# Loading the pooling weights sooner and closing a gate's sums later in a hybrid transformer block

## The chip, the cores and the metric

The kernel runs on one core of a Trainium2 chip. The metric is the time of one execution on the device in microseconds (us); the median of several runs is used. All times inside an execution are counted from the start of its span, the stretch from its first to its last recorded instruction.

## The reference

One layer of a backbone works on 1024 latent tokens and 256 context tokens with 1024 features each, in 32-bit floats. What matters here:

```python
mod_x = silu(c) @ w_mod + b_mod                  # shifts, scales and gates: sh1 sc1 gt1 sh2 sc2 gt2
h_x, h_c = modulate(x, ...), modulate(ctx, ...)  # normalised, scaled, shifted
u, q, k, v = split(h @ w_in)                     # 512 columns each; k and v for the context as well
d = [window_mean(u_g, w) - u_g for w in (2, 4, 8, 16)]       # four groups of 128 channels
y = (d_g @ pool_w_g) * pool_scale                # a 128 x 128 weight per group
attn = neighbourhood_attention(q, k, v, k_ctx, v_ctx, rpb)   # 8 heads, softmax over a window and the context
mix = concat([y, attn]) @ w_out
x = x + gt1 * rmsnorm(mix, g_post_mix)           # the first gate
x = x + gt2 * rmsnorm(sq_relu_mlp(...), g_post_mlp)          # the second gate
```

The window means near both ends of the sequence have smaller counts; their reciprocals are the "table of ends".

## The kernel before

Every large product is made of three matmuls: each factor is split into a high part (a rounded copy, made by ScalarE, L146 or L148) and a low part (the rest, made by VectorE, L152 or L154), and L198, L199 and L200 multiply high by high, high by low and low by high. A weight's way is therefore: a DMA into one of four buffers ("raw"), a high part on ScalarE, a low part on VectorE, then its matmuls. Pages of 128 x 1024 floats come from a common pool of 33.

The stages that matter are these.

- Startup (up to L693): tokens are normalised and transposed, the pooling input u is projected, and the keys of the context are made (tiles `pkc`, copied by L690 to `kcT`). The last statement splits the values' weights `wv0` to `wv3`, whose DMAs were issued one by one as raw buffers came free. Inside this stage the order on TensorE, ScalarE, VectorE, SyncE's queue and GpSimd is the written order (`in_order`). Just ahead of the keys stand the loads of the pooling weights `pwt` (256 KB) and of the table of ends `edg` (32 KB), L636 to L640.
- The context's values (L731 to L743, tiles `pvc`), and then the latent tokens' values (`pv`). Between them VectorE makes the pooling differences (`pooled`, L643) and sums rows of the modulation (`accsh`, `accsc`), ScalarE splits the pooling weights into `pwh` and `pwl` (L739), and the pooling products follow (`py`). What stands in the block at L731 is only bound to come behind the last VectorE instruction of the startup.
- The query and key products (L916 to L946), in written order again. A part of this is the first gate: rows of `w_mod` are summed into `acca` on VectorE, then at step 17 `mod_gate` loads the gain `gpa` by four DMAs on SyncE's queue, sums over partitions with eight small matmuls (L236, tile `pga`) and multiplies (L244); `mod_out` sends the row out by four DMAs on GpSimd's queue (L250). Step 20 then calls `tables(0)`: its source is loaded as `U0w`, and GpSimd builds the bias tables for the first pair of heads out of it (L872).
- The attention, 32 units in rounds `i` (L1150 on), in written order on all engines. A round makes scores on TensorE (L978), adds bias and takes the minimum on VectorE (L992), the exponentials on ScalarE (L1001), transposes, and sums of values (L1054) for earlier units. `tables(1)` is called in round 2. The gate is read back as a page at round 30 (`gate_page`).
- The output projection, the MLP and the second gate, at whose start `mod_gate("b", ...)` loads a gain and closes the sums as well (L1869).

Of the kernel before, what the change touches and what calls it, by code (L numbers as in the profile page):

```python
# [18 lines left out]
P = 128  # L19
# [61 lines left out]
def hybrid_block(ctx, tc, x, ctx_in, w_mod, b_mod, gp1, gp2, w_in, pool_w, rpb, w_out, w1, w2, vectors,  # L81
# [94 lines left out]
    def load(name, src):  # L176
        raw = wraw.tile([P, 1024], F32, tag="raw", name=f"{name}w")
        nc.sync.dma_start(raw.rearrange("p (a b) -> p a b", b=src.shape[-1]), src)
        return raw
# [7 lines left out]
    def add_to(to, more):  # L187
        nc.gpsimd.dma_start(to, more, accum_op=add)

    def pair(w, kk, c0, n):  # L190
        return w[2 * kk * P : (2 * kk + 2) * P, c0 : c0 + n].rearrange("(a p) f -> p a f", p=P)
# [41 lines left out]
    def mod_sums_of(name, acc, bank):  # L233
        ps = bank(f"pg{name}")
        for c in range(4):
            nc.tensor.matmul(ps[32 * c : 32 * c + 32, :256], ones[:, :32], acc[:, c * 256 : (c + 1) * 256],  # L236
                             start=True, stop=True)
        return ps[:, :256]

    def mod_gate(name, acc, gp, bank, g):  # L240
        quarters = gp.rearrange("(c o f) -> c o f", c=4, o=1)
        for c in range(4):
            nc.sync.dma_start(g[32 * c : 32 * c + 32, :], quarters[c].to_broadcast([32, 256]))
        nc.vector.tensor_tensor(acc[:, :256], mod_sums_of(name, acc, bank), g, mul)  # L244


    def mod_out(name, acc):
        gates[name] = dram.tile([1, D], F32, tag=f"g{name}", name=f"g{name}")
        for c in range(4):
            nc.gpsimd.dma_start(gates[name][:, c * 256 : (c + 1) * 256], acc[32 * c : 32 * c + 1, :256])  # L250
# [17 lines left out]
    with tc.tile_pool(name="ps1", bufs=6, space=PSUM) as ps1, tc.tile_pool(name="tmp1", bufs=3) as tmp:  # L268

        def bank(name):  # L270
            if name[:2] == "pm" or name in ("pxt1_0", "pxt0_2", "pxt1_7", "pct2", "pct3"):
                return lasting(name)
            return ps1.tile([P, 512], F32, tag="mm", name=name)

        def once(name, shape):
            return tmp.tile(shape, F32, tag=name, name=name, bufs=1)
# [224 lines left out]
            return high_low(f"{name}{kk}", raw[kk], 1.0 if kk < 2 else -1.0)  # L501

        raw_k = [load(f"wk{kk}", pair(w_in, kk, 1024, 512)) for kk in range(KT // 2)]

# [126 lines left out]
        ctx_tok = lambda i: lambda k: (hc[k][0][:, i * P : (i + 1) * P], hc[k][1][:, i * P : (i + 1) * P])  # L633
        lat_tok = lambda b, i: lambda k: (hx[b][k][:, i * P : (i + 1) * P], hx[b][k][:, 512 + i * P : 512 + (i + 1) * P])

        pwt = once("pwt", [P, 4, P])  # L636
        nc.sync.dma_start(pwt, pool_w.rearrange("g c d -> c g d"))
        pwh, pwl = (tmp.tile([P, 512], F32R, tag=f"pw{n}", name=f"pw{n}", bufs=1) for n in "hl")
        edg = once("edg", [P, 4, 16])
        nc.sync.dma_start(edg, edge.rearrange("o (g e) -> o g e", g=4).to_broadcast([P, 4, 16]))  # L640
        dT = []

        def pooled(g, up):  # L643
# [84 lines left out]
        vcp = page("vc")  # L728
        pool_order = in_order(ET.Pool)
        pool_order.__enter__()  # L730
        with tc.issue_after(last[ET.DVE]):  # L731
            for i in range(2):
                ps = bank(f"pvc{i}")
                token_group(ps, wgt, ctx_tok(i))
                nc.scalar.copy(vcp[:, i * 512 : (i + 1) * 512], ps)
                if i == 0:
                    difference(1)
                    split(pwt.rearrange("p g d -> p (g d)"), pwh, pwl)
                    difference(2)  # L739
                else:  # L740
                    difference(3)
                background(2)
# [177 lines left out]
        with in_order(ET.PE, ET.Pool, ET.Activation, ET.DVE, ET.SP) as pooling:  # L920
            banks = {of: [bank(f"p{of}{j}") for j in range(2)] for of in "KQ"}
            use(-1)
            for step, (n, of, j) in enumerate([(n, of, j) for n, of in products for j in range(2)]):
                half_product(n, of, j, banks[of])
                use(step)
                if step in (5, 9, 17):
                    name = {5: "S1", 9: "S4", 17: "S3"}[step]
                    parts = token_operand(name, sraw[name])
                if step in (5, 7, 9, 11, 17, 19):
                    next(parts)  # L930
                    next(parts)
                if step in (7, 11):
                    name = {7: "S4", 11: "S3"}[step]
                    sraw[name] = token_raw(name)
                if step == 5:
                    column_sums("sc", accs["sc"], scale2)
                if step == 17:
                    mod_gate("a", accs["a"], gp1, bank, tmp.tile([P, 256], F32, tag="mrow", name="gpa", bufs=2))
                    mod_out("a", accs["a"])
                if step == 14:  # L940
                    mask_page()
                if step == 20:
                    tables(0)
                if step in (21, 22):
                    for g in range(2):
                        pool_mixed(2 * (step - 21) + g)  # L946
                kept_product(n, of, j, banks[of][j])


    with (  # L950
# [195 lines left out]
        with in_order(ET.PE, ET.Activation, ET.DVE, ET.SP) as projected:  # L1146
# [7 lines left out]
            for i in range(N + 4):  # L1154
                if i < N and units[i][1] == 2 and units[i][0] < 3:
                    tables(units[i][0] + 1)
                if i in LOADS:
                    weight_load(0, kks[LOADS.index(i)])
                if i == N:
                    t1 = [out_load(f"to1_{kk}w", kk, 1) for kk in (0, 1)]  # L1160
                    b22 = [out_load(f"bo22_{kk}w", kk, 1) for kk in (2, 3)]
                    t3 = [out_load(f"to3_{kk}w", kk, 1) for kk in (2, 3)]
                    for to, kk in zip(t1, (0, 1)):
                        add_to(halved(to), out_block(kk, 0))
                if i == N - 2:
                    G1 = gate_page("a")
                if i > 3:
                    weighed(i - 4)
                    if i % 8 == 3:
                        j = i // 8 - 1  # L1170
                        add_to(s1a[j], heads[j][:, 512:])
                        add_to(sa2[j], heads[j][:, 512:])
                if i in (1, 2):
                    with tc.issue_after(pooling[ET.Pool]):
                        for k in (2 * i - 2, 2 * i - 1):
                            add_to(s3[k], s1a[k])
                if i in (5, 6):
                    for k in (2 * i - 10, 2 * i - 9):
                        nc.sync.dma_start(sa2[k], s3[k])
                if 8 < i < N and i % 8 == 7:  # L1180
                    j = i // 8 - 1
                    add_to(heads[j][:, :512], sa2[j])
                low()
                if i > 0 and i % 8 == 0:
                    mixed_split(i // 8 - 1)
                for n, at in enumerate(HALVES):
                    if at == i:
                        weight_split(n)
                if i < N:
                    scores(i)  # L1190
                else:

                    t = i - N
                    if t == 0:
                        x, s1 = [], halves_of("so1_")
                    if t % 2 == 0:
                        xs = ps_s.tile([P, 1024], F32, tag="S", name=f"pox{t}")
                        x += [xs[:, :512], xs[:, 512:]]
                    out_sums(x[t], "A11", wo, t, True)
                    nc.scalar.copy(s1[t], x[t])  # L1200
                if 1 < i <= N + 1:
                    turn(i - 2)
                    fifth_kept(i - 2)
                if i < N:
                    exps(i, 0)
                if 1 < i <= N + 1:
                    turn_kept(i - 2, 0, nc.scalar.copy)
                if i < N:
                    exps(i, 1)
                if 1 < i <= N + 1:  # L1210
                    turn_kept(i - 2, 1, nc.vector.tensor_copy)
                if i < 2:
                    last_query("P4", i)
                if 0 < i <= N:
                    share(i - 1)
                if 2 < i <= N + 2:
                    values(i - 3)
                if i > N:
                    out_operand("S1", i - N - 1, s1a[i - N - 1])
# [25 lines left out]
    with tc.tile_pool(name="ps2", bufs=6, space=PSUM) as ps2:  # L1245
# [6 lines left out]
      with ExitStack() as tmp2:  # L1252
# [550 lines left out]
        with tc.issue_after(first[ET.PE]), in_order(ET.PE, ET.Activation, ET.DVE, ET.SP):  # L1803
# [59 lines left out]


            pg = bank("pgb")
            x = four("pyx")
            for g in range(NG):
                if g == 2:
                    acc = acc_b[-1]  # L1869
                    mod_gate("b", acc, gp2, lambda name: pg, tmp.tile([P, 256], F32, tag="gp", name="gpb", bufs=1))  # L1870
                    mod_out("b", acc)
                group(x, "P1", g)
            s1 = halves("s1")
            for t in range(4):
# [82 lines left out]
```

## Time and profile before

| | us |
|---|---|
| median of 3 runs | 1038.9 |
| lowest and highest | 1038.55, 1040.34 |
| the profiled execution | 1039.78 |
| its span | 1038.0 |
| TensorE busy | 1020.5 |
| VectorE busy | 755.6 |
| ScalarE busy | 543.5 |
| GpSimd busy | 107.8 |

In a profile PE is TensorE, PEld its loading of weights, ACT ScalarE, DVE VectorE, POOL GpSimd, SPq SyncE's queue. A row of the timeline gives start, duration, engine, line, operation, tile written and tiles read, shapes and count; in square brackets stands how long the engine was idle before it and who ended that. A row of the waits gives who waited for whom, the time in total, how often, and the longest. A row of the windows gives the stretch, its length, the busy time of each engine with the number of instructions, the granted clock of TensorE (1.00 is full speed), the busy share of the DMA engines and GB/s.

### The profile page before, as it was taken

To read this page: it belongs to the slowest core of one execution; us is meant where nothing else is said; L and a number is where in the kernel's file an instruction comes from. 1 tells how busy PE (TensorE), PEld (TensorE's weight loads), DVE (VectorE), ACT (ScalarE), POOL (GpSimd) and SP (SyncE) were. 2 spreads that over 40 slices of the span, in tenths; PEclk is the share of its full clock that TensorE was granted. 3 is DMA by queue.
4 is the path that set the end of the run, shared out by engine and by line. 5 is a ranking of instruction groups with operands and counts; after the bars stand their busy time and mean duration, and the time that the engine had idled before them with its cause. 6 is when DMAs were issued, how large, how long until landed. Compare 5 with 4: busy or idle time off the path is not lost.

```text
span 1038.0 us, 15636 instructions
## 1 busy us (share of the span) xinstructions
PE 1020.5 (98%) x5814; PEld 837.2 (81%) x5814; DVE 755.6 (73%) x1183; ACT 543.5 (52%) x941; POOL 107.8 (10%) x163
## 2 busy tenths in 40 slices
PE   8998999999999999999999999999999999999997
PEld 6787888877878888887888888888888888888885
DVE  5586937688997598868998888754586666547586
ACT  7572254318887556876555544544453334334431
POOL 3011121071211302310000000000000000000001
PEclk9998999999999999999999999999999999999999
DMA  9999598831337786794776657635698766545556
GB/s 341 329 246 339 191 228 291 277 81 62 72 93 193 167 189 203 225 254 164 258 267 222 213 203 226 210 112 206 239 335 277 235 233 221 203 175 193 174 185 206
DMA packets 122908, 221.63 MB, mean 214 GB/s; under 512 B 9424, under 2 KB 55248, under 8 KB 122832
## 3 DMA queue, kind: packets, MB, share of 16 engines
q1 hardware_dynamic: 96608, 170.75, 50.0%
q0 software_dynamic: 9088, 18.92, 9.4%
q10 hardware_dynamic: 17136, 30.97, 8.0%
q8 instruction: 45, 0.74, 0.3%
q14 instruction: 31, 0.25, 0.1%
HBM read 167.63 MB, written 51.92 MB: 212 GB/s over the span
## 4 chain that ended last, share of the span: by engine, by line
PE 92%; DMA 2%; ACT 2%; DVE 2%; issue 1%; SPq 0%; POOL 0%; DVEq 0%; POOLq 0%; ACTq 0%
PE S L978 3%; PE pa L1054 3%; PE phz L198 3%; PE phv L198 3%; PE phx L198 3%; PE pyx L198 3%; PE phx L199 3%; PE phx L200 3%; PE pyx L199 3%; PE phz L200 3%; PE pyv L199 3%; PE pyv L198 3%; PE pyz L199 3%; PE pyz L198 3%; PE pyx L200 3%; PE phv L200 3%
## 5 line engine op out<-in xcount | busy, mean ns | idle before, releaser
L1001 ACT ACTIVATE sp<-sp,nm 128x640 f32<-128x640 f32 (+1 forms) x64 | 51.4, 802 | 19.1 <-DVE nm L992 18.5
L1558 ACT ACTIVATE c<-c 128x512 f32<-128x512 f32 x48 | 30.3, 632 | 48.5 <-DVE c L1678 25.0
L146 ACT CAST wpS<-S 128x512 fp32r<-128x512 f32 x64 | 38.8, 616 | 27.9 <-PE phv L200 9.9
L198 PE MATMUL phx<-thB,wpA 128*128 128x512 f32 x128 | 50.2, 392 | 0.0
L200 PE MATMUL phx<-thB,wpA 128*128 128x512 f32 x128 | 49.9, 389 | 0.0
L199 PE MATMUL phx<-tlB,wpA 128*128 128x512 f32 x128 | 49.8, 389 | 0.0
L152 DVE TENSOR_TENSOR wpS<-S,wpS 128x512 fp32r<-128x512 f32 x64 | 43.4, 685 | 8.2 <-ACT wpS L146 8.2
L992 DVE CUSTOM_DVE_ANT_0 sp<-S,tab 128x640 f32<-128x640 f32 (+1 forms) x56 | 42.9, 803 | 8.5 <-PE S L978 6.8
L1559 ACT ACTIVATE c<-c 128x512 f32<-128x512 f32 x48 | 30.3, 631 | 14.4 <-DVE sa L1641 13.6
L140 POOL TENSOR_TENSOR ry<-vy,nhalf 128x1 f32<-128x1 f32 x8 | 4.4, 550 | 280.8 <-DVE vy L138 280.8
L198 PEld LDWEIGHTS phx<-thB,wpA 128*128 128x128 f32 x128 | 24.0, 188 | 5.5 <-ACT s L1609 0.5
L978 PE MATMUL S<-kT,q 64*128 64x384 f32 (+1 forms) x128 | 27.8, 495 | 0.3 <-DVE nm L992 0.3
L200 PEld LDWEIGHTS phx<-thB,wpA 128*128 128x128 f32 x128 | 24.0, 188 | 5.0
L199 PEld LDWEIGHTS phx<-tlB,wpA 128*128 128x128 f32 x128 | 24.0, 188 | 4.8
L1054 PE MATMUL pa<-pt,v 128*64 128x128 f32 x352 | 25.9, 280 | 0.7 <-ACT px L1034 0.2
L1039 DVE COPY pt<-T 128x512 f32<-128x512 f32 x32 | 22.0, 686 | 5.5 <-PE T L1020 5.5
L198 PE MATMUL phz<-thB,wpS 128*128 128x512 f32 x64 | 25.0, 391 | 0.0
L198 PE MATMUL phv<-thT,wpA 128*128 128x512 f32 x64 | 25.0, 391 | 0.0
L199 PE MATMUL phz<-tlB,wpS 128*128 128x512 f32 x64 | 24.9, 390 | 0.0
L199 PE MATMUL phv<-tlT,wpA 128*128 128x512 f32 x64 | 24.9, 389 | 0.0
L200 PE MATMUL phz<-thB,wpS 128*128 128x512 f32 x64 | 24.9, 389 | 0.0
L198 PE MATMUL phy<-thT,wpS 128*128 128x512 f32 x64 | 24.9, 389 | 0.0
(1104 smaller groups left out, 3382.3 us busy)
## 6 DMA issues: line engine op xcount, KB each, us to landing
b<-in_w SPq DMA_DIRECT2D x64, 512.0 KB, 4.2
hrS<-hdS SPq DMA_DIRECT2D x32, 512.0 KB, 5.4
hrA<-hdA SPq DMA_DIRECT2D x24, 512.0 KB, 5.6
wm<-in_w_mod SPq DMA_DIRECT2D x16, 512.0 KB, 9.7
wa_0w<-in_w SPq DMA_DIRECT2D x16, 512.0 KB, 5.1
wa_1w<-in_w SPq DMA_DIRECT2D x16, 512.0 KB, 4.3
hdA<-c ACTq DMA_DIRECT2D x32, 256.0 KB, 2.3
hdS<-sa ACTq DMA_DIRECT2D x32, 256.0 KB, 2.3
```

What stands on the lines that cost most here:

```text
L146: nc.scalar.copy(hi, src)
L152: nc.vector.tensor_tensor(lo, src, hi.bitcast(F32), sub)
L198: nc.tensor.matmul(ps, ahi, bhi, start=first, stop=False, skip_group_check=more)
L199: nc.tensor.matmul(ps, ahi, blo, start=False, stop=False, skip_group_check=more)
L200: nc.tensor.matmul(ps, alo, bhi, start=False, stop=last, skip_group_check=more)
L978: nc.tensor.matmul(S[e][:, c0 : c0 + keys.shape[1]], q[hs, cols], keys[hs], start=True, stop=True)
L992: nc.vector.tensor_tensor_reduce(out=to, in0=s, in1=bt, scale=1.0, scalar=BIG, op0=add, op1=ALU.min, accum_out=nm)
L1001: nc.scalar.activation(sp, sp, AF.Exp, bias=least[i, e], scale=-1.0, accum_out=sums[i][:, e : e + 1])
L1039: copy(turns[i].rearrange("p e i t -> p (e i) t")[:, :, h * HD : (h + 1) * HD], turned[i][h].rearrange("p (a t) -> p a t", a=8))
L1054: nc.tensor.matmul(pa[e * HD : (e + 1) * HD, cols], v[:, f : f + HD], turns[i][:, e, c] if c < 4 else fifths[i][:, :, (e + 1) * HD : (e + ...
L1558: nc.scalar.activation(r, src, AF.Relu)
L1559: nc.scalar.activation(r, r, AF.Square)
```

## The change

Four edits:

- The loads of `pwt` and `edg` are issued right behind the keys' weights in the startup, instead of ahead of the keys' products.
- The instructions of the block at L731 must now also come behind the last ScalarE instruction of the startup, which is the high part of `wv3`. The split of `pwt` is among them.
- `mod_gate` no longer loads its gain; `mod_gain` does. The first gate's gain is loaded in attention round 0, and the sums are closed in round 4 into the free half of the bank `pz`; step 17 of the products is empty of them.
- The second gate's gain is loaded just ahead of the first groups, not at the third.

```diff
+    def mod_gain(gp, g):
         quarters = gp.rearrange("(c o f) -> c o f", c=4, o=1)
         for c in range(4):
             nc.sync.dma_start(g[32 * c : 32 * c + 32, :], quarters[c].to_broadcast([32, 256]))
+        return g
+
+    def mod_gate(name, acc, g, bank):
         nc.vector.tensor_tensor(acc[:, :256], mod_sums_of(name, acc, bank), g, mul)
...
         raw_k = [load(f"wk{kk}", pair(w_in, kk, 1024, 512)) for kk in range(KT // 2)]
+        pwt, edg = once("pwt", [P, 4, P]), once("edg", [P, 4, 16])
+        nc.sync.dma_start(pwt, pool_w.rearrange("g c d -> c g d"))
+        nc.sync.dma_start(edg, edge.rearrange("o (g e) -> o g e", g=4).to_broadcast([P, 4, 16]))
...
-        pwt = once("pwt", [P, 4, P])
-        nc.sync.dma_start(pwt, pool_w.rearrange("g c d -> c g d"))
-        edg = once("edg", [P, 4, 16])
-        nc.sync.dma_start(edg, edge.rearrange("o (g e) -> o g e", g=4).to_broadcast([P, 4, 16]))
...
-        with tc.issue_after(last[ET.DVE]):
+        with tc.issue_after(last[ET.DVE]), tc.issue_after(last[ET.Activation]):
...
-                if step == 17:
-                    mod_gate("a", accs["a"], gp1, bank, tmp.tile([P, 256], F32, tag="mrow", name="gpa", bufs=2))
-                    mod_out("a", accs["a"])
...
+                if i == 0:
+                    gain = mod_gain(gp1, att.tile([P, 256], F32, tag="gp", name="gpa"))
+                if i == 4:
+                    mod_gate("a", accs["a"], gain, lambda name: pz[:, 256:])
+                    mod_out("a", accs["a"])
...
+            gain = mod_gain(gp2, tmp.tile([P, 256], F32, tag="gp", name="gpb", bufs=1))
             x = four("pyx")
             for g in range(NG):
                 if g == 2:
-                    mod_gate("b", acc, gp2, lambda name: pg, tmp.tile([P, 256], F32, tag="gp", name="gpb", bufs=1))
+                    mod_gate("b", acc_b[-1], gain, lambda name: pg)
```

More of the change, by code (lines that the diff above doesn't have):

```diff
@@ L238, in mod_sums_of @@
         return ps[:, :256]
-    def mod_gate(name, acc, gp, bank, g):
+    def mod_gain(gp, g):
         quarters = gp.rearrange("(c o f) -> c o f", c=4, o=1)
@@ L1868, in hybrid_block @@
                 if g == 2:
-                    acc = acc_b[-1]
-                    mod_gate("b", acc, gp2, lambda name: pg, tmp.tile([P, 256], F32, tag="gp", name="gpb", bufs=1))
-                    mod_out("b", acc)
+                    mod_gate("b", acc_b[-1], gain, lambda name: pg)
+                    mod_out("b", acc_b[-1])
                 group(x, "P1", g)
```

## The prediction

> **What bounds the kernel now.** I read the page first: busy shares and granted clock.
>
> ```profile
> PE 1020.5 (98%) x5814; PEld 837.2 (81%) x5814; DVE 755.6 (73%) x1183; ACT 543.5 (52%) x941; POOL 107.8 (10%) x163
> PEclk9998999999999999999999999999999999999999
> ```
>
> TensorE is busy for nearly all of the span, so an edit is worth what it takes from TensorE's waits and from matmuls that run slower than they could. One slice, the fourth (78 to 104 us), has a lower clock. The list of TensorE's waits, longest first, begins with what stands there:
>
> ```profile
> PE pvc L198 <- ACT wv0h L146: 3.7, 1, 3.7
> ```
>
> The longest single wait is for the high part of the first values' weight. Ahead of it, the chain of work that ended last, in order of time, has two transfers:
>
> ```profile
> 74.74 7.16 DMA wv0w<-in_w_in
> 81.92 7.79 DMA pwt<-in_pool_w
> ```
>
> The raw data of `wv0` had landed at 81.9; the pooling weights landed at 89.7, and only then did ScalarE go on. Its timeline, and that of TensorE, say why:
>
> ```profile
> 89.74 0.62 ACT L146 CAST pwh<-pwt 128x512 fp32r<-128x512 f32 x1 [6.91 <-DMA pwt<-in_pool_w]
> 90.26 0.64 ACT L690 COPY kcT<-pkc 128x256 f32<-128x256 f32 x2
> 90.79 1.06 ACT L146 CAST wv0h<-wv0w 128x1024 fp32r<-128x1024 f32 x1
> 91.73 1.05 ACT L146 CAST wv1h<-wv1w 128x1024 fp32r<-128x1024 f32 x1
> 87.90 0.28 PE L200 MATMUL pkc<-hc,wk3l 128*128 128x256 f32 x1
> 91.90 1.22 PE L198 MATMUL pvc<-wv0h,hc 128*128 128x512 f32 x2 [3.72 <-ACT wv0h L146]
> 97.06 0.40 PE L199 MATMUL pvc<-wv1l,hc 128*128 128x512 f32 x1
> 98.21 0.39 PE L198 MATMUL pvc<-wv2h,hc 128*128 128x512 f32 x1
> 100.93 0.39 PE L199 MATMUL pvc<-wv0l,hc 128*128 128x512 f32 x1
> ```
>
> ScalarE works in order. The split of `pwt`, whose products come only behind the first values' in the code, stands ahead of the last two copies of `kcT` and of all four `wv` splits, and waits 6.91 us for its DMA. TensorE has nothing else to do. The last four rows show a second cost: from 91.90 to 97.06 twelve matmuls were started in 5.16 us, from 98.21 to 100.93 twelve took 2.72. The windows give the clock:
>
> ```profile
> 4.74:8.15 3.41, 1.89 (x18) 1.65 (x16) 2.05 (x11) 3.18 (x6) 1.25 (x2) 1.00 1.02 416
> 88.20:90.07 1.87, 0.00 (x0) 0.00 (x0) 0.06 (x1) 0.33 (x1) 0.95 (x1) 1.00 1.04 365
> 90.07:91.90 1.83, 0.00 (x1) 0.00 (x1) 0.28 (x3) 1.83 (x5) 1.66 (x3) 0.50 1.02 377
> 91.90:96.90 5.00, 5.00 (x12) 3.98 (x13) 5.00 (x7) 2.79 (x3) 0.57 (x1) 0.50 1.04 222
> ```
>
> The clock halved 1.87 us into the wait and came back at 96.90, 6.83 us later.
>
> **Part 1, the wait.** With the split of `pwt` behind `wv3`'s high part, ScalarE has only the copies of `kcT` before `wv0h`. TensorE's last key product ends at 87.90 + 0.28 = 88.18; the last copy follows about 0.05 later, as TensorE followed `wv0h` (90.79 + 1.06 = 91.85, then 91.90); two copies and then `wv0h` start 0.27 apart (90.26, 90.79 for the two), so `wv0h` starts at about 88.5. TensorE started 91.90 - 90.79 = 1.11 after it, so at 89.6: the wait is 1.4 instead of 3.7, and 2.3 us are gone. Nothing new is late: `wv3`, issued last, lands in time by
>
> ```profile
> 80.06 0.37 SPq L178 DMA_DIRECT2D wv3w<-in_w_in  x1
> DMA to landing us min/median/max: 7.4/7.4/7.4
> ```
>
> at 87.5, and its turn on ScalarE is 88.5 + 3 x 0.95 = 91.4. VectorE's low part of `wv0` would start 1.1 after `wv0h`, at 89.6, and end 1.2 later at 90.8; six matmuls that need no low part stand ahead of the first that does (two of `pvc`, four of `pv`, in the order of now) and end at 89.6 + 6 x 0.227 = 91.0. It just fits; if the order of TensorE changes so that only two stand there, it costs up to 0.8.
>
> **Part 2, the clock.** Of the 3.41 us up to the fall at 90.07, 1.87 were idle, 55%. In the stretch from 4.74 to 8.15, equally long, TensorE was busy for 1.89, so 1.52 were idle, 45%, and the clock stayed at 1.00. A wait of 1.4 us is at most 41% of any such stretch, less than what it bore, so I take the clock to stay full. That returns 5.16 - 2.72 = 2.44 us. The other bound is nothing returned, if the row of 4.74, which holds only transposes, says little of matmuls.
>
> The Trainium skill (TensorE: Matmul & The Clock Gate, "What's actually happening") has free-running windows of 3.4 us and a fall to half clock after at least one idle window. The length agrees, 6.83 being two such windows, but the trace falls after 1.87 us of idling, so here a full idle window was not needed. By that rule a wait of 1.4 us never halves the clock, and the sum is the same. The same page, "PE-mode transpose", says that transposes do not count as busy; the full clock at 4.74 to 8.15 speaks against it.
>
> **Part 3, the moved loads.** `pwt` and `edg` (288 KB) go to about 53 us on SyncE's queue. TensorE waits for no DMA anywhere in its list, and what they are moved past are copies to DRAM and stored sums, read after 83 us at the earliest, as well as the `wv` loads, which find the queue emptier. I take nothing; the ends are the 0.8 us that 288 KB take at the 365 GB/s of that stretch, either way, hidden by the 3.9 us for which `wv3w` would lie ready.
>
> **Part 4, VectorE behind it.** VectorE's stretch from the low parts to the pooling splits starts with `wv0l`, so it moves by 2.3 us only, while TensorE moves by 4.7.
>
> ```profile
> 91.88 1.23 DVE L152 TENSOR_TENSOR wv0l<-wv0w,wv0h 128x1024 fp32r<-128x1024 f32 x1 [1.51 <-ACT wv0h L146]
> 106.50:127.00 20.50, 20.50 (x92) 16.77 (x90) 19.07 (x37) 4.28 (x8) 0.34 (x1) 1.00 0.59 185
> 123.20 1.28 DVE L223 SCALAR_TENSOR_TENSOR accsh<-wmsh_7w,sx,accsh 128x1024 f32<-128x1024 f32 x1
> 127.16 0.57 PE pgsh L236 x8
> ```
>
> The sums `accsh` are ready at 124.5, TensorE wants them at 127.1. Of these 2.6 us 2.4 go, so the two would meet within 0.2. This is the tightest place: VectorE is busy 19.07 of 20.50 there. I put 0.1 to it; its ends are 0 and, if VectorE keeps none of its gain, 2.1.
>
> **Part 5, the first gate.** The products lose eight small matmuls, and VectorE a wait; GpSimd loses the gate's four DMAs, which stood ahead of the bias tables:
>
> ```profile
> 205.02 0.64 PE L236 MATMUL pga<-acca,ones 128*32 128x256 f32 x8
> 207.54 0.43 DVE L244 TENSOR_TENSOR acca<-pga,gpa 128x256 f32<-128x256 f32 x1 [2.15 <-DMA gpa<-in_gp]
> 208.26 1.94 POOL L250 DMA_DIRECT2D ga<-acca  x4 [28.74 <-DVE acca L244]
> 210.72 7.52 POOL L872 TENSOR_TENSOR tab<-msk,U0w 128x128 f32<-128x128 f32 x12
> 218.94 7.04 DVE L154 SCALAR_TENSOR_TENSOR mix<-y,mix 128x512 fp32r<-128x512 f32 x2 [1.45 <-ACT mix L148]
> 219.91 5.52 POOL L872 TENSOR_TENSOR tab<-msk,U 128x128 f32<-128x128 f32 x12
> 225.91 1.27 DVE L912 TENSOR_TENSOR kT<-pK,kT 128x512 f32<-128x512 f32 x2
> 227.58 0.70 PE L978 MATMUL S<-kcT,q 64*128 64x256 f32 x4
> 738.53 2.68 SPq L243 DMA_DIRECT2D gpb<-in_gp  x4
> 215.00:310.00 95.00, 94.12 (x1222) 75.26 (x1222) 81.05 (x214) 68.21 (x181) 28.22 (x54) 1.00 0.33 78
> ```
>
> TensorE saves 0.57 here (the chain's price for the eight matmuls of `pgsh`, which are alike) and pays as much in round 4, in a stage where it is busy 94.12 of 95.00. VectorE's 0.43 stands there ahead of round 4's minima and delays them while TensorE is held by the same sums: between -0.6 (all hidden in the rounds' small waits) and +0.5 (0.64 and 0.43 in a row, less 0.57); I take 0. The gain's four DMAs have four rounds to land in, the gate is read back 26 rounds later, and what GpSimd has next behind it is the tables of round 10.
>
> ```profile
> 201.73 1.24 SPq L865 DMA_DIRECT2D U0w<-in_rpb  x2
> DMA to landing us min/median/max: 5.9/5.9/5.9
> ```
>
> What hangs on this part is where the first scores can start. Two `mix` splits of VectorE take 7.04 us while GpSimd builds tables; behind them the two sums of `kT` end at 227.18, 0.4 ahead of the scores at 227.58. If this chain stayed where it is, TensorE, 4.7 us sooner, would wait 4.3 and the gain would be lost here. It does not stay: its other inputs are products, which move with TensorE, and GpSimd's part starts without the wait for the gate. `U0w` was issued at 201.73 behind the gain's DMAs and landed 5.9 later at 207.6; the tables start at 210.7. So they can come 3.1 us sooner on top of the shift. I take nothing lost; the upper end is 0.2 (the 0.57 saved here less the 0.4 of room).
>
> **Part 6, the second gate's gain.** Its four issues (738.53, 2.68 us) go ahead of a few loads of weights on SyncE's queue, and the sums' multiply finds it landed. TensorE's list has no wait in that stage; I take nothing, at worst the 2.7.
>
> **The sum.** The profiled execution took 1039.78 us (span 1038.0 and 1.78 around it). 1039.78 - 2.3 - 2.44 + 0.1 = 1035.14; I round up, to 1035.2, since what I took at nothing can mostly cost. The median before is 1038.9: the profiled run is 0.9 above it, which fits a clock that fell and came back at other moments in other runs (one of the two slow stretches instead of both would cost 1.2 less; the lowest run, 1038.55, is 1.2 below the profiled one). What I remove is the profiled run's own loss, so 1035.2 holds for the medians too, 0.36% below. About 0.2%, some 2 us, is what a measurement of this kernel can tell from no change.
>
> ```profile
> L154 DVE SCALAR_TENSOR_TENSOR mix<-y,mix x4: 743/1202/5657, 214.7 to 220.3; 128x512 fp32r<-128x512 f32 x4
> 210.21 1.73 DVE L152 TENSOR_TENSOR S3h<-S3r,S3h 128x512 fp32r<-128x512 f32 x2
> 211.17 0.39 PE L198 MATMUL pK<-S3h,wKT3h 128*128 128x512 f32 x1
> L200 PE MATMUL pqv<-hx,wQT4l x8: 388/389/389, 229.2 to 235.5; 128*128 128x512 f32 x8
> ```
>
> **Rivals.** (a) *The clock still falls* on the shorter wait. For: only one bearing row, and of transposes. Against: it bore more idling. Only 2.3 us are gained: 1037.4, within 0.2% of the median.
>
> (b) *VectorE becomes the bound* between 90 and 127 us, or at 210 us, and takes back part. For: the margin of 0.2. Against: it has 1.43 us of slack in 20.50. Price 0.5 to 2.1: 1035.7 to 1037.3. A second form: GpSimd's tables, 3.1 us sooner, run beside the splits of `S3h` (210.21), as the longest `mix` split ran beside tables and took 5.66 us. Locked out until twelve tables at the 0.46 of the second set end, at 207.6 + 5.5 = 213.1, the two splits end at 214.5 for products that begin at 211.17 and reach the third quarter of `S3h`, for which they are, 6 matmuls of 0.227 later at 212.5: 0.7 for the first split and no more than 2 for both. The Trainium skill (SBUF — State Buffer, "Terms") says that VectorE and GpSimd share a port pair exclusively and that the loser fully blocks; the 5.66 agrees.
>
> (c) *Slower: the gate's row keeps its page.* `acca` now holds one of 33 pages until round 4. Should the second pair of tables want that page, it takes another, at worst one that the last query products (`pqv`) read until 235.5. Twelve tables (5.5 or 7.5) and the gate's four issues (1.9) behind them then end at 242.9 to 244.9 and land up to 5.9 later, by 249 to 251, and only then is the gate's page free. It decides if a copy of round 4 is given that page. Those products fill rounds 0 and 1, about 3 us each, so round 4's copies are due near 243 and would wait 6 to 8: 1041 to 1043; from a wait of 5.8 on it is slower. Against: by the code eight pages are free again by round 2.
>
> (d) *It does not do what it says*: the `wv` splits find another cover, such as raw data landing later behind the moved loads. Then 1038 to 1040.
>
> **Chances.** Forecast 0.64, (a) 0.08, (b) 0.15, (c) 0.10, (d) 0.03. Faster by over 0.2% (below 1036.8): the forecast and two thirds of (b), 0.74. Within 0.2%: (a), a third of (b), (d), 0.16. Slower by over 0.2%: (c), 0.10. The range goes from 1034.0 (Part 5's gain of 0.6, and 0.6 for runs) to 1037.6, over the forecast, (a) and (b).
>
> **What would show it.** TensorE's wait for `wv0h` at 1.4; `pwh` behind `wv3h`; no window of half clock near 92; the values' first product at 89.6, and the scores' first at about 222. Wrong would be: half clock after 89.6, TensorE waiting at `pgsh`, at `S3h`, at the first scores or in round 4.

## The result: slower, and the profile after

The changed kernel takes 1043.87 us (median of 6 runs, 1043.55 to 1044.6), the kernel before beside it 1039.47 (6 runs, 1038.52 to 1040.35): a ratio of 1.0043, 95% interval 1.003 to 1.0056. The forecast was 1035.2, in a range from 1034.0 to 1037.6. The sign was wrong: 0.36% faster was forecast, 0.43% slower was measured.

Most of what it said of the first 700 us is in the profile all the same. TensorE's timeline where the values begin and ScalarE's beside it, the windows there, and TensorE at the first scores and in round 4, all of the kernel after:

```profile
88.16 0.37 ACT L692 COPY kcT<-pkc 128x256 f32<-128x256 f32 x1 [2.50 <-PE pkc L200]
88.43 1.05 ACT L146 CAST wv0h<-wv0w 128x1024 fp32r<-128x1024 f32 x1
92.23 0.60 ACT L146 CAST pwh<-pwt 128x512 fp32r<-128x512 f32 x1
89.53 0.72 PE L198 MATMUL pvc<-wv0h,hc 128*128 128x512 f32 x2 [1.41 <-ACT wv0h L146]
...
92.00:96.00 4.00, 4.00 (x19) 3.32 (x18) 4.00 (x18) 0.84 (x2) 0.77 (x1) 1.00 0.92 243
...
222.10 0.70 PE L977 MATMUL S<-kcT,q 64*128 64x256 f32 x4
236.31 0.64 PE L236 MATMUL pz<-acca,ones 128*32 128x256 f32 x8
```

`pwh` stands behind the values' splits, the wait is 1.41 in place of 3.72, the first product starts at 89.53 (89.6 was forecast), the clock (last number but two of the window) is 1.00, the scores start at 222.10 ("about 222"). The same step of ScalarE, far down the program, is 4.86 us sooner than before; the first row is of the kernel before, the second of the one after:

```profile
719.37 0.63 ACT L1558 ACTIVATE c<-c 128x512 f32<-128x512 f32 x1 [2.80 <-DVE c L1678]
```
```profile
714.51 0.63 ACT L1563 ACTIVATE c<-c 128x512 f32<-128x512 f32 x1 [2.80 <-DVE c L1683]
```

Then all of it is lost, and more, within 30 us. TensorE's list of waits after has a new head, in the stage where the forecast said that there is no wait:

```profile
PE pyx L198 <- ACT b_3h L146: 5.5, 1, 5.5
PE pyx L199 <- DVE b_3l L152: 0.7, 1, 0.7
```

The timelines of SyncE's queue, before and then after, say where it comes from. Each row is an issue; `b` is a weight and `hrA` an operand of one group, loaded back from `hdA`, where it was stored in DRAM (`hdS` is a second place of this kind). So the rows go group by group:

```profile
715.43 0.37 SPq L1705 DMA_DIRECT2D b<-in_w  x1
724.43 0.34 SPq L1721 DMA_DIRECT2D hrA<-hdA  x1
724.88 0.38 SPq L1705 DMA_DIRECT2D b<-in_w  x1
736.22 0.34 SPq L1721 DMA_DIRECT2D hrA<-hdA  x1
```
```profile
705.51 0.34 SPq L1726 DMA_DIRECT2D hrA<-hdA  x1
733.46 1.73 SPq L243 DMA_DIRECT2D gpb<-in_gp  x4
735.30 0.38 SPq L1710 DMA_DIRECT2D b<-in_w  x1
735.73 0.47 SPq L1726 DMA_DIRECT2D hrA<-hdA  x1
```

Before, the weight of the third group (counted from 0) goes out at 715.43 and the gain `gpb` behind the fourth group, at 738.53. After, the gain stands ahead of the third group's loads, waits until 733.46, and the weight goes out at 735.30: 19.9 later, although ScalarE's step above is 4.9 sooner. ScalarE's split and the clock follow:

```profile
740.66 1.04 ACT L146 CAST hhA_3h<-hrA 128x1024 fp32r<-128x1024 f32 x1 [10.87 <-DMA hrA<-hdA]
742.70 0.79 PE L198 MATMUL pyx<-b_3h,hhA_3h 128*128 128x512 f32 x1 [5.52 <-ACT b_3h L146]
744.15 0.80 PE L199 MATMUL pyx<-b_3l,hhA_3h 128*128 128x512 f32 x1 [0.66 <-DVE b_3l L152]
...
737.18:741.06 3.88, 0.00 (x1) 0.00 (x0) 0.00 (x0) 0.40 (x1) 0.00 (x0) 1.00 1.04 402
741.06:747.88 6.82, 4.52 (x10) 3.27 (x11) 5.77 (x6) 5.38 (x6) 0.51 (x2) 0.50 1.04 404
```

The account: 4.86 ahead, 5.52 + 0.66 = 6.18 of waiting, and 4.52 us of products at half clock, of which I count half, 2.26, as lost. That is 3.6 behind; the spans differ by 1041.9 - 1038.0 = 3.9.

### The profile page after: what moved, and what is told of

Read it like the earlier page. It is cut to its first block, busy times and chain, and to the rows that moved or that the text cites. A ratio compares the mean times of both kernels' runs of the same rounds, so it can differ in the third digit from the quotient of the medians.

```text
span 1041.9 us, 15640 instructions
## 1 busy us (share of the span) xinstructions
PE 1021.6 (98%) x5814; PEld 838.0 (80%) x5814; DVE 755.9 (73%) x1183; ACT 544.0 (52%) x941; POOL 108.3 (10%) x163
## 4 chain that ended last, share of the span: by engine, by line
PE 92%; ACT 2%; DMA 2%; DVE 2%; issue 1%; SPq 0%; ACTq 0%; DVEq 0%; POOLq 0%
PE pu L449 4%; PE S L977 3%; PE pa L1053 3%; PE pyv L199 3%; PE pyz L199 3%; PE pyv L200 3%; PE pyz L200 3%; PE pyz L198 3%; PE pyv L198 3%; PE phx L198 3%; PE phx L199 3%; PE phx L200 3%; PE phv L198 3%; PE phz L198 3%; PE phv L199 3%; PE phz L199 3%
## 5 line engine op out<-in xcount | busy, mean ns | idle before, releaser
L198 PE MATMUL phv<-thT,wpA 128*128 128x512 f32 x64 | 25.0, 391 | 0.0
L200 PE MATMUL phv<-thT,wpA 128*128 128x512 f32 x64 | 24.9, 389 | 0.0
```

What stands on the lines that cost most here:

```text
L198: nc.tensor.matmul(ps, ahi, bhi, start=first, stop=False, skip_group_check=more)
L200: nc.tensor.matmul(ps, alo, bhi, start=False, stop=last, skip_group_check=more)
```

## The experiments

Times are medians. The kernel before took 1039.34 beside e1 to e4, 1039.65 beside e10 and e6 to e8, 1039.32 beside e5, e9, e11 and e12.

**Is the loss in the second gain alone?** e1 puts only this part back:

```diff
-            gain = mod_gain(gp2, tmp.tile([P, 256], F32, tag="gp", name="gpb", bufs=1))
             x = four("pyx")
             for g in range(NG):
                 if g == 2:
+                    gain = mod_gain(gp2, tmp.tile([P, 256], F32, tag="gp", name="gpb", bufs=1))
                     mod_gate("b", acc_b[-1], gain, lambda name: pg)
```

> The changed kernel, with one part undone: the second gate's gain (gpb) is loaded again where it was, behind the loads of the third and fourth group. Theory: the whole loss lies in that one move. Its four DMA issues now stand in SyncE's in-order queue at 733.46, ahead of b_3 (735.30) and hrA_3 (735.73); TensorE then waits 5.5 for b_3h and runs at half clock from 741.06 to 747.88. Up to round 4 the changed kernel was 4.9 us ahead of the kernel before; with the move undone that lead should last to the end: 1039.5 - 4.9 = 1034.6, between 1034.0 and 1035.6. The trace should show the lead of 4.9 also behind 740, the wait of pyx for b_3h at 0 and no half clock near 741. Rival 1, the lead collides in any case: groups three and four come 4.9 sooner, while hdA's stores and loads are paced by transfers, so a wait near 740 stays also without the move; then 1037 to 1041. Rival 2, the loss is in the parts ahead of it (the clock, the first gate in round 4): then about 1043, as the changed kernel.

Measured: 1035.03 (1034.63 to 1036.59), ratio 0.9959 [0.9946, 0.9971]. TensorE's list has no wait behind 700. e2 does this part alone, in the kernel before (its diff is e1's the other way round):

> The kernel before, with only the second gate's gain moved ahead of the loads of the third and fourth group; nothing else of the change. Theory: the four issues hold the queue until the old readers of the tile's memory are done, b_3 and hrA_3 go out late, TensorE waits 5 to 6 and the clock halves for some 7 us (2.3 to 3.4 more): 1039.5 + 8 = 1047.5, between 1044.5 and 1049. In the trace pyx waits for b_3h, with half clock behind it. Rival, the loads were only late because everything ahead of them came 4.9 sooner in the changed kernel: then here the issues find their readers done, and the cost is at most the 2.7 of four issues: 1039.5 to 1042.

Measured: 1048.14 (1046.79 to 1048.98), ratio 1.0081 [1.0068, 1.0095]; TensorE waits 5.3 and 0.7 there. The part costs 1043.87 - 1035.03 = 8.8 with the rest of the change and 1048.14 - 1039.34 = 8.8 without it. Both rivals fall: the loss doesn't come from being early, and no other part has a share that shows.

**Why do the issues hold the queue?** The tile of `gpb` is the first in a pool of memory that the stage before has just given up, and some of what read that memory (its old readers) is still under way. In the changed kernel one wait of SyncE's queue from 705 to 740 stands out, for a store that reads the old pool:

```profile
SPq L243 <- DMA hdA<-c: 27.4, 1, 27.4
```

e3 gives the tile memory of its own, at the same place of the program:

```diff
-            gain = mod_gain(gp2, tmp.tile([P, 256], F32, tag="gp", name="gpb", bufs=1))
+            gain = mod_gain(gp2, cst("gpb", [P, 256]))
```

> The changed kernel with the second gain in memory of its own that nothing else ever uses; the four issues stay where the change puts them, ahead of the loads of the third and fourth group. Theory: what held the queue until 733.46 was the wait for the last readers of the memory under gpb (the stores of hdA from c among them, landing 2.75 after 730.53); without an old reader the issues go out at once and only their own time, four by 0.4 to 0.7, is left in the queue, well ahead of the loads. 1034.6, between 1034.0 and 1036. Rival, the four issues themselves cost it (their time in the queue, or their packets ahead of the loads on the DMA engines): then the wait for b_3h stays at 3 to 5.5 and the time at 1041 to 1044.

Measured: 1042.38 (1041.75 to 1044.47), ratio 1.003 [1.002, 1.004]. My theory fell here: without an old reader TensorE's wait for `b_3h` went from 5.5 to 3.8 only. The rival's figures came true, but not its first reason: the four issues take 0.31 to 0.41 each. Its second, the packets, falls with e10 below. The timeline of e3, and the three longest waits of SyncE's queue from 705 to 733:

```profile
710.86 21.01 SPq L243 DMA_DIRECT2D gpb<-in_gp  x4
732.38 0.39 SPq L1710 DMA_DIRECT2D b<-in_w  x1
```
```profile
SPq L243 <- DMA hdS<-sa: 10.9, 1, 10.9
SPq L243 <- DMA hdA<-r: 8.7, 1, 8.7
SPq L243 <- DMA b<-in_w: 4.5, 1, 4.5
```

The four issues now stretch over 21 us, and wait for a load and two stores with which they share neither tile nor memory. The program's list of instructions shows what they do share (HW5 and so on are completion counters; of the kernel e3, then of e1):

```
gpb<-in_gp    [waits HW5]
gpb<-in_gp    [waits HW6]
gpb<-in_gp    [waits HW7]
gpb<-in_gp    [waits HW0]
b_3<-in_w     [waits HW1, SW5, PE]
hrA_3<-hdA_3  [waits HW2, DVE]

b_3<-in_w     [waits HW5, SW5, PE]
hrA_3<-hdA_3  [waits HW6, DVE]
b_4<-in_w     [waits HW7, SW0, PE]
hrA_4<-hdA_4  [waits HW0, DVE]
```

In these programs the issues of SyncE and ScalarE together take eight counters in turn, and each first waits until the transfer that had its counter before has landed. The four issues of the gain stepped into the counters of `b_3` to `hrA_4`, and so into their waits; the loads came behind. In the changed kernel the first issue waits for the old pool's readers as well, until 733.46; with the counters alone, in e3, the fourth goes out at 731.6. So the two holds end about 2 us apart. By the addresses in the changed kernel's program, the store that is waited for reads a tile of the old pool of which `gpb` covers no byte: here the first tile of a new pool waits also for readers of other bytes of the old one.

The kernel before has the same three waits as e3; the list of the waits of its SyncE queue from 707 to 742:

```profile
SPq L1721 <- DMA hdS<-sa: 11.2, 2, 10.9
SPq L1721 <- DMA hdA<-r: 8.6, 1, 8.6
SPq L1705 <- DMA b<-in_w: 4.5, 1, 4.5
```

There the long one, 10.9, falls on the load of the fourth group, which has the time. e4, whose expectation is older than e3's result, takes the four issues off this queue, memory and place as in the change:

```diff
-    def mod_gain(gp, g):
+    def mod_gain(gp, g, queue=nc.sync):
...
-            nc.sync.dma_start(g[32 * c : 32 * c + 32, :], quarters[c].to_broadcast([32, 256]))
+            queue.dma_start(g[32 * c : 32 * c + 32, :], quarters[c].to_broadcast([32, 256]))
...
-            gain = mod_gain(gp2, tmp.tile([P, 256], F32, tag="gp", name="gpb", bufs=1))
+            gain = mod_gain(gp2, tmp.tile([P, 256], F32, tag="gp", name="gpb", bufs=1), nc.gpsimd)
```

> The changed kernel with the second gain's four DMAs issued from GpSimd's queue; same tile in the same memory, at the same place of the program. Theory: the wait for the memory's old readers is still there, but no load stands behind it on SyncE's queue, so b_3 and hrA_3 go out as they did before the change: 1034.6, between 1034.0 and 1036.5 (what GpSimd has behind the wait may come a little later). Rival, the wait is not in the queue but in the loads themselves (hrA_3 is late since hdA's store is late, whatever stands ahead): then pyx waits 4 to 5.5 here too and the time is 1041 to 1044.

Measured: 1035.29 (1035.23 to 1035.55), ratio 0.996 [0.9947, 0.9972]; the issues stand on GpSimd at 734.55, and nobody is late. So the wait itself costs nothing where nothing urgent is queued behind it. But e4 can't tell memory from counters. e10 can: e3 with one issue in place of four.

```diff
-            gain = mod_gain(gp2, cst("gpb", [P, 256]))
+            gain = cst("gpb", [P, 256])
+            nc.sync.dma_start(gain, gp2.rearrange("(c o f) -> c o f", c=4, o=1).to_broadcast([4, 32, 256]))
```

> The kernel of e3 (the second gain in memory of its own, ahead of the loads of the third and fourth group), but its four issues made one, which writes all 128 rows. e3 has shown that the issues wait also without an old reader: for the landing of b_2, of two stores of hdA and of one of hdS, one each, and the fourth at 731.56. New theory: the issues of SyncE and ScalarE take eight completion counters in turn, and each waits for the landing of the transfer that had its counter before; four issues push the loads four counters on, so that b_3 meets the counter that hrA_4 met in e1 and waits until 731.6. One issue pushes them by one: gpb at about 710.9, b_3 at 719.9, hrA_3 at 720.3, b_4 at 731.6; hrA_3 is then 1 us later than in e1 and TensorE waits for nothing: 1035.0, between 1034.4 and 1036. Rival 1, a load of the gain at this place costs it whatever its form: 1041 to 1043.5. Rival 2, a shift by one already brings back a wait below 1.5: 1036 to 1038.

Measured: 1035.49 (1034.93 to 1038.55), ratio 0.9958 [0.9944, 0.9972]. The profiled execution is the longest of the five; it lost its 3 us at 464, in a stage that the edit doesn't touch, so its rows count from one another:

```profile
714.28 0.65 SPq L1872 DMA_DIRECT2D gpb<-in_gp  x1
723.03 0.38 SPq L1710 DMA_DIRECT2D b<-in_w  x1
723.51 0.41 SPq L1726 DMA_DIRECT2D hrA<-hdA  x1
734.72 0.37 SPq L1710 DMA_DIRECT2D b<-in_w  x1
```

The third group's loads leave 9 us behind the gain and ahead of the long wait, as expected; rival 1 falls, and rival 2 would need 1036 or more. The same bytes to the same memory at the same place cost 7 us in four issues (e3), and nothing that shows in one.

e11 leaves it at four issues and moves them to round 0, into memory of their own:

```diff
                     gain = mod_gain(gp1, att.tile([P, 256], F32, tag="gp", name="gpa"))
+                    gainb = mod_gain(gp2, cst("gpb", [P, 256]))
...
-            gain = mod_gain(gp2, tmp.tile([P, 256], F32, tag="gp", name="gpb", bufs=1))
...
-                    mod_gate("b", acc_b[-1], gain, lambda name: pg)
+                    mod_gate("b", acc_b[-1], gainb, lambda name: pg)
```

> The changed kernel with the second gain in memory of its own, loaded by four issues in the first attention round, right behind the first gain, some 500 us ahead of its use. Theory: four issues cost only where the loads behind them are the next that TensorE needs and the counters that they meet belong to late stores; in round 0 the loads behind them are tables for later rounds. b_3, hrA_3, b_4 and hrA_4 then meet the counters that they meet in e1: 1035.0, between 1034.4 and 1036. Rival, the shift by four meets a late transfer there too and a round waits: 1036 to 1039.

Measured: 1034.79 (1034.56 to 1034.85), ratio 0.9956 [0.9944, 0.9969]. The same four issues into memory of their own cost 7 us ahead of the third group's loads and nothing here: what is queued behind them decides, not the load.

**What made the gain that e1 keeps?** e7 undoes the first gate's move, so that of the change only the first edit is left:

```diff
+                if step == 17:
+                    mod_gate("a", accs["a"], mod_gain(gp1, tmp.tile([P, 256], F32, tag="mrow", name="gpa", bufs=2)), bank)
+                    mod_out("a", accs["a"])
...
-                if i == 0:
-                    gain = mod_gain(gp1, att.tile([P, 256], F32, tag="gp", name="gpa"))
-                if i == 4:
-                    mod_gate("a", accs["a"], gain, lambda name: pz[:, 256:])
-                    mod_out("a", accs["a"])
```

> The kernel of e1, with the first gate's sums back at step 17 and its gain loaded there, as in the kernel before; so only the first edit of the change is left. Theory: the gate's move was worth nothing (predicted: 0, at best 0.6), since the products that the chain towards the scores needs come sooner with TensorE: e1 + 0 to 0.6, 1035.0 to 1035.6. Rival, GpSimd's tables and VectorE's chain stay late without the move, and the first scores wait: they start at 222.1 in the changed kernel and would start up to 4.3 later, 1036 to 1039.3.

Measured: 1034.78 (1034.7 to 1035.09), ratio 0.9954 [0.9941, 0.9967], as e1. The move is worth nothing that shows. e5 and e6 halve the first edit, loads alone and order alone:

```diff
-        with tc.issue_after(last[ET.DVE]), tc.issue_after(last[ET.Activation]):
+        with tc.issue_after(last[ET.DVE]):
```

> The kernel of e1 without the order on ScalarE: the pools' small weights and the table of ends are loaded sooner, and nothing holds the split of pwh back. Put together so, pwh stands on ScalarE beside the splits of hx_6 and hx_7, 30 us ahead of the values' weights, near the time when pwt lands (57.4 in the changed kernel); the copies of kcT and the splits of wv0 to wv3 then follow one another as in e1. Theory: what counts is that nothing stands between the last kcT copy and wv0h; the wait is 1.4 here too, and 0.6 for pwh is hidden by ScalarE's slack near 57: 1035.0, between 1034.6 and 1036. Rival, ScalarE waits there for pwt or the 0.6 delays hx_7, and TensorE with it: up to 1.0 more, 1036.

```diff
         raw_k = [load(f"wk{kk}", pair(w_in, kk, 1024, 512)) for kk in range(KT // 2)]
-        pwt, edg = once("pwt", [P, 4, P]), once("edg", [P, 4, 16])
-        nc.sync.dma_start(pwt, ...)
-        nc.sync.dma_start(edg, ...)
...
+        pwt, edg = once("pwt", [P, 4, P]), once("edg", [P, 4, 16])
+        nc.sync.dma_start(pwt, ...)
+        nc.sync.dma_start(edg, ...)
         pwh, pwl = (tmp.tile([P, 512], F32R, tag=f"pw{n}", name=f"pw{n}", bufs=1) for n in "hl")
```

> The kernel of e1, with the pools' small weights and the table of ends loaded at their old place again, and ScalarE's order as changed (the split of pwh behind those of the values' weights). Theory: the two parts of the first edit need one another. The order alone takes the wait from 3.7 to 1.4; but the small transfers land near 90, and VectorE's pwl (or what takes edg) stands ahead of the split wv0l, so the low halves come up to 1 us later: e1 + 0.4 to 1.1, 1035.4 to 1036.2. Rival 1, the moved loads are worth nothing: the time of e1, 1035.0 within 0.4. Rival 2, the longer wait halves the clock again: e1 + 2.4 and the rest of the wait, 1037.5 to 1039.5.

Measured: e5 1034.73 (1034.5 to 1034.88), ratio 0.9956 [0.9943, 0.9968]; e6 1035.74 (1035.32 to 1036.45), 0.9963 [0.995, 0.9976]. Each half alone takes the wait to 1.4 and brings nearly all. In e6 VectorE does wait for the ends' table as expected, and its first low part starts at 89.91 (89.50 in the changed kernel):

```profile
89.61 0.16 DVE L670 TENSOR_TENSOR ed<-ed,edg 128x1 f32<-128x1 f32 x1 [7.26 <-DMA edg<-in_edge]
89.91 1.23 DVE L152 TENSOR_TENSOR wv0l<-wv0w,wv0h 128x1024 fp32r<-128x1024 f32 x1
```

Whether the time pays for it stays open: the intervals of e1, e5 and e6 overlap.

**Is the clock a cost of its own?** e8 and e12 leave the wait of the kernel before as it is, and fill it with transposes that nobody reads (20, then 34):

```diff
+        dummy = bank("pvc_dummy")
+        spare(dummy[:, :P], 20)
         startup.close()
```

> The kernel before, with 20 transposes more on TensorE ahead of its wait for wv0h, into a bank that nobody reads; the wait for the split stays until about 93 us. Theory: of the gain of the first edit, 2.3 is the wait and 2.44 the stretch at half clock from 90.07 to 96.90 behind it. Twenty transposes by some 0.11 fill 2.2 of the wait of 3.7; the clock then doesn't fall: 1039.3 - 2.4 = 1036.9, between 1036.5 and 1038.2 (the transposes may run over the wait's end). In the trace the first products after the wait take 0.23 each, not 0.43. Rival 1, the clock falls all the same: 1039 to 1040. Rival 2, the clock's fall cost nothing of its own, since what came behind it waits for loads: 1039.3.

Measured: 1039.32 (11 runs, 1037.47 to 1040.47), ratio 0.9995 [0.9986, 1.0004]: no difference shown, and the median lies outside what I expected. But the profiled execution, at 1037.65, has no stretch at half clock there, and 1.44 of the wait was left open; four runs lie near 1037.6, seven from 1038.9 up.

> The kernel of e8 with 34 transposes in place of 20, so that they fill the whole of the wait for wv0h (0.117 each: 4.0). In e8 1.44 and 0.53 of idle time were left, and its times fell into two groups, four near 1037.6 at a granted clock of 0.998 to 0.999 and seven near 1039.6 at 0.996 to 0.997. Theory: the clock's fall behind the wait costs 2 to 2.4 by itself, and the idle time left decided in which executions it fell; with none left nearly all lie near 1037.5, between 1037.0 and 1038.2, at 0.998 or more. Rival, the second group comes from somewhere else: then it stays, and the median is 1038.5 to 1039.8.

Measured: 1038.25 (11 runs, 1037.53 to 1038.56, granted clock 0.997 to 0.999), ratio 0.999 [0.9981, 0.9999]. The upper group is gone, and no run has a lower granted clock than 0.997, where the 15 runs of the kernel before have 0.994 to 0.997. So the clock does cost time by itself, and filling the wait keeps it up; but the interval only just leaves out no difference. The timeline and the windows of e12:

```profile
87.97 3.87 PE L338 MATMUL pvc_dummy<-ident 128*128 128x128 f32 x34
91.70 0.49 PE L198 MATMUL pvc<-wv0h,hc 128*128 128x512 f32 x1
92.96 0.50 PE L199 MATMUL pvc<-wv0l,hc 128*128 128x512 f32 x1 [0.76 <-DVE wv0l L152]
...
88.20:91.60 3.40, 3.40 (x34) 3.40 (x32) 0.32 (x2) 2.06 (x5) 2.51 (x4) 1.00 1.05 355
91.60:96.90 5.30, 4.54 (x21) 3.47 (x20) 5.22 (x7) 2.91 (x4) 0.68 (x1) 1.00 1.05 249
```

The gain is 1.1 by medians and 1.8 by the profiled spans (1038.0 and 1036.2), less than the 2.44 of the stretch: at full clock TensorE comes too soon for `wv0l` and waits 0.76, which the slow products had hidden. The median is 0.7 above the 1037.5 that I expected, just outside the range.

**A version that beats both.** e9 is e1 with the high parts of two values' weights ahead of the last copy of `kcT`. That copy waits for the keys' last product on TensorE; the high parts need not:

```diff
-            if k == KT - 1:
+            if k == KT - 1 and j < 3:
                 nc.scalar.copy(kc[:, j], pkc[j])
...
-        wgt = [in_weights("wv", raw_v, kk) for kk in range(KT // 2)]
+        wv = [in_weights("wv", raw_v, kk) for kk in range(2)]
+        nc.scalar.copy(kc[:, 3], pkc[3])
+        wgt = wv + [in_weights("wv", raw_v, kk) for kk in range(2, KT // 2)]
```

> The kernel of e1, with the splits wv0h and wv1h ahead of the last kcT copy on ScalarE. In e1 they stand behind that copy, which waits for the last product of the keys (88.16), and so TensorE, done with the keys, waits the 1.4 of kcT and wv0h. Theory: ScalarE is idle from 85.65 to 88.16, wv0h starts as soon as the keys' readers of its memory are done, near 86, and the wait of 1.4 goes: 1035.0 - 1.4 = 1033.6, between 1033.0 and 1034.4. Rival, the wait moves to wv0l or wv1l on VectorE, whose splits take 1.22 each: up to 1.0 stays, 1034.6.

Measured: 1033.37 (1033.14 to 1033.58), ratio 0.9943 [0.993, 0.9955]. ScalarE and TensorE in e9:

```profile
85.92 1.05 ACT L146 CAST wv0h<-wv0w 128x1024 fp32r<-128x1024 f32 x1 [0.23 <-PE pkc L199]
86.87 1.04 ACT L146 CAST wv1h<-wv1w 128x1024 fp32r<-128x1024 f32 x1
88.20 0.37 ACT L699 COPY kcT<-pkc 128x256 f32<-128x256 f32 x1 [0.29 <-PE pkc L200]
...
88.00 0.39 PE L198 MATMUL pvc<-wv0h,hc 128*128 128x512 f32 x1
```

The wait is gone, and no other took its place in TensorE's list behind 80. Of e5 and e11, measured beside it and with the wait of 1.4, no run is below 1034.5.

## Why the prediction was wrong

**Part 6 failed, and alone turned the sign.** It priced the second gain's four issues by the time that they take (2.68) and called the stage free of waits. "A few loads of weights" were the loads of the next two groups, of which the third is due at 741.88 before. What the issues wait for was not asked, and no rival had it. That the queue waits there was to be read: the waits of SyncE's queue before, shown above, are 4.5, 8.6 and 10.9 long; that an issue ahead takes them over is shown by e3's list of counters. The place between the pools, with the old readers, stood in the code. The runs show 8.8 in place of 0 to 2.7: 6.2 of TensorE's waiting and some 2.3 of half clock, 0.4 not placed.

Two things held the issues: the old pool's readers until 733.46 in the changed kernel, and the counters until 731.6 in e3. Without the old readers (e3) TensorE's wait was 3.8 + 0.9 rather than 5.5 + 0.7, and the counters alone still cost 7.35 (1042.38 - 1035.03). What the old readers cost alone, with one issue in the old pool's memory, was not run, so how the 8.8 is shared between the two stays open.

**The other parts hold.** With Part 6 taken out, the sum of 1035.2 stands against 1035.03 (e1). Part 1 is right to 0.1. Part 2 is right that the clock stays full; e1's gain of 4.3 less the 2.3 of the wait leaves 2.0 for the 2.44 that I put. Part 3 (nothing): e5 has the loads sooner and loses nothing that shows. Part 4: TensorE takes `pgsh` at 122.4, 4.7 sooner, and its list shows no wait there; the sums end at 121.7, so 0.7 was left where 0.2 was forecast. Part 5 (nothing): e7 shows no worth of the move.

**The rivals.** None of the four came true: the clock held at 92, no wait appeared at `pgsh`, at the first scores or in round 4, and the first edit did what it says. The slower rival sought its mechanism, a buffer that is not yet free, at the first gate; it was a near relation of that, at the second. The list of what would make the forecast wrong did not name that stage.

## What to carry to other kernels

Before an issue is moved ahead on a DMA queue that keeps its order, read what the queue itself waits for in that stretch, and when the data of the loads behind it is due; the issue's own duration says little. Issues take completion counters and memory as well as time: count them (one issue in place of four), put early loads where what follows is not urgent, and give them memory without old readers. Here a wait of 3.7 or 5.5 us on TensorE cost its length and a stretch at half clock behind it; one of 1.4 cost its length alone.

## What the runs showed of the hardware

The clock fell 3.88 us into the wait that began at 737.18 and was low for 6.82, as it was for 6.83 at 90.07 before, where 1.87 us had been enough. In e10's profiled execution a wait of 1.8 that ended at 465.9 was enough as well (2.00 us with 0.59 busy, then 3.80 at a mean of 0.55). The wait of 1.41 in the changed kernel left it at 1.00.

```profile
464.50:466.50 2.00, 0.59 (x3) 0.50 (x4) 1.74 (x2) 2.00 (x4) 0.00 (x0) 1.00 0.11 39
466.50:470.30 3.80, 3.80 (x11) 2.98 (x10) 2.99 (x5) 2.39 (x4) 0.00 (x0) 0.55 0.00 1
```

In e12 transposes through the whole wait kept the clock at 1.00. The Trainium skill (TensorE: Matmul & The Clock Gate, "PE-mode transpose") says that the full clock does not engage for transposes, since they do not count as busy in the same way. For keeping the clock up e12 speaks against it: the window that holds nothing else is at 1.00, and so is the one behind it.
